# Loading the prompt as features by tokens, and dropping its transposes on TensorE

## The chip, the cores and the metric

The kernel runs on one core of a Trainium2 chip. The time is the device time of one execution in microseconds (us); for the kernel before the change it is the median of three runs, 3384.19 us (3377.82 to 3388.36). The engines are named as the profile names them: PE (TensorE; PEld is its weight load), DVE (VectorE), ACT (ScalarE), POOL (GpSimd) and SP (SyncE, which here only issues DMAs).

## The reference, cut to what matters

One inference step of a hybrid decoder layer. A prompt of 4096 tokens of 1024 features is normalised, multiplied by a weight of 1024 x 3072, and the twelve column blocks of the product feed four branches (a diagonal state-space model, a gated convolution, stick-breaking attention, attention to memory tokens). Beside it runs a decoding step of 8 x 4 tokens over a paged cache.

```
def rmsnorm(x, g):
    y = xf * lax.rsqrt(jnp.mean(xf * xf, axis=-1, keepdims=True) + EPS)
    return y * g
h = rmsnorm(x, lp["norm_g"]) @ lp["w_in"]
(a_u, a_g, b_b, b_c, b_x, b_g, c_q, c_k, c_v, c_g, m_q, m_g) = jnp.split(h, N_IN_BLOCKS, axis=-1)
```

The change concerns only how `rmsnorm(x, norm_g)` of the prompt comes to stand where the matrix product reads it.

## The kernel before, in words

The first stage projects the prompt. It goes through eight chunks of 512 tokens; within a chunk it goes through 24 units, one for each 128 of the 3072 output features. A unit (`part`, `proj`, L211 to L223) is 24 matmuls of 128 x 128 weights on 512 tokens: for each of eight 128-feature blocks `hi*hi` (L218), `hi*lo` (L219) and `lo*hi` (L220), since weights and input are each split in a rounded part and its remainder. The weights of unit i come by one DMA of 512 KB (`stg`, L204, two buffers), ACT copies the rounded part (`whl<-stg`, L42), and DVE subtracts it to make the remainder (`whl<-stg,whl`, L45, "the low part" below). The first L220 of a unit cannot start before that subtraction is done. The DMA for unit i+2 and the ACT copy for unit i+1 are issued in unit i.

The order on every engine is the order in which the program is written; nothing reorders it. `proj` calls `between` three times in a unit. `between` first runs what stands in the list `soon` (small pieces of work that were put off), then at most one of the low parts, then `slot`, which advances the decoding step and other background generators. So the projection's matmuls, the decoding step (`dz`, `dO`, `dwT`, cache loads `kt` from POOL's queue and `vt` from SP's queue) and the branches (`nat`, `pT`, `mo` and others) lie interleaved on all engines.

The input must stand with features on the 128 partitions, in a buffer `xh` (rounded part and remainder, 8 blocks, 512 tokens). Before the change the prompt is loaded as it lies, 128 tokens by 1024 features (`x_load`, L188, units 14 to 17 of the chunk before). `x_stats` (units 17 to 20) squares it on ACT in two halves that also give the sums, and scales it on DVE by the token's factor and the feature's weight (L179). `x_split` then transposes four 128 x 128 pieces on PE (L195) into a PSUM tile of the pool `tr` (two buffers, shared with `bc`, `yT`, `nat` and others), ACT copies the rounded part into `xh`, and DVE subtracts. There are eight such splits for a chunk, put between the matmuls of units 22 and 23 of the chunk before and units 0 and 1 of the chunk.

The second stage (from about 2000 us) is the attention over the prompt and the output projection; the change does not touch it.

Of the kernel before, what the change touches and what calls it, by code (L numbers as in the profile page):

```python
# [2 lines left out]

# [5 lines left out]
F32 = mybir.dt.float32  # L9
F32R = mybir.dt.float32r  # L10
I32 = mybir.dt.int32
AF = mybir.ActivationFunctionType
ALU = mybir.AluOpType
# [4 lines left out]
SEQ, DM, GW = 4096, 1024, 256  # L18
KT = DM // 128
CH = 512  # L20
NCH = SEQ // CH
EPS = 1e-6
A_U, A_G, B_B, B_C, B_X, B_G, C_Q, C_K, C_V, C_G, M_Q, M_G = range(12)

def dap(ap, off, dims):
    return bass.AP(tensor=ap.tensor, offset=ap.offset + off, ap=dims)
# [2 lines left out]
@with_exitstack  # L29
def hymba_kernel(ctx: ExitStack, tc: tile.TileContext, x_p, x_s, cache_k, cache_v, s_re, s_im, s_conv,  # L30
                 cmem_k, cmem_v, ptab, mem_p, norm_g, w_in, w_out, gng, lam_re, lam_im, b_re, b_im,
                 c_re, c_im, log_dt, ssm_d, w_glu, conv_w, sb_bias, w_mem, fin_g,
                 o_yp, o_ys, o_k, o_v, o_hre, o_him, o_conv, o_mk, o_mv, o_sk, o_sv,
                 o_shre, o_shim, o_sconv):
    nc = tc.nc
# [2 lines left out]
    mm, tr = nc.tensor.matmul, nc.tensor.transpose  # L38
    V, S, P, SP = nc.vector, nc.scalar, nc.gpsimd, nc.sync

    def act(out, in_, f=AF.Copy, **kw):
        return S.activation(out, in_, f, **kw)  # L42

    def tt(eng, out, a, b, op):
        return eng.tensor_tensor(out=out, in0=a, in1=b, op=op)  # L45

    cst = ctx.enter_context(tc.tile_pool(name="cst", bufs=1))
# [16 lines left out]
    ident = cst.tile([128, 128], F32, name="ident")  # L64
    jmat = cst.tile([128, 128], F32, name="jmat")
    ones32 = cst.tile([128, 32], F32, name="ones32")
    nhalf = cst.tile([128, 8], F32, name="nhalf")
    sel = cst.tile([128, 2], F32, name="sel")
    sgn = cst.tile([128, 1], F32, name="sgn")
    gnc = cst.tile([128, 8], F32, name="gnc")  # L70
    cwc = cst.tile([128, 2, 3], F32, name="cwc")
    b4 = cst.tile([128, 4], F32, name="b4")
    nb4 = cst.tile([128, 4], F32, name="nb4")
# [37 lines left out]
    sb = p1.enter_context(tc.tile_pool(name="sb1", bufs=1))  # L111
# [3 lines left out]
    def ev(dt=F32, name="ev"):  # L115
        return sb.tile([128, 512], dt, tag="ev", name=name, bufs=5)
# [7 lines left out]
    def trp(name="trp"):  # L124
        return ps.tile([128, 4, 128], F32, tag="tr", name=name, bufs=2)
# [45 lines left out]
    def x_stats(x, n=128, then=lambda f: f()):  # L171

        ss = sb.tile([128, 4], F32, tag="ss", name="ss", bufs=4)
        for k in range(2):
            act(ev()[0:n], x[0:n, k * 512:(k + 1) * 512], AF.Square, accum_out=ss[0:n, k:k + 1])
        tt(V, ss[0:n, 0:1], ss[0:n, 0:1], ss[0:n, 1:2], ALU.add)
        V.tensor_scalar(ss[0:n, 0:1], ss[0:n, 0:1], 1.0 / DM, EPS, op0=ALU.mult, op1=ALU.add)
        tt(P, ss[0:n, 2:3], ss[0:n, 0:1], nhalf[0:n, 0:1], ALU.pow)
        then(lambda: V.scalar_tensor_tensor(x[0:n], x[0:n], ss[0:n, 2:3], ngr[0:n], op0=ALU.mult, op1=ALU.mult))  # L179

    xq = {}

    def x_tile(name="xt", dt=F32):
        return sx.tile([128, DM], dt, tag="xt", name=name, bufs=4)

    def x_load(i):
        xq[i] = x_tile()
        SP.dma_start(xq[i], x_p[0, i * 128:(i + 1) * 128, :])  # L188

    def x_split(i, k4):  # L190
        xs = xq[i]
        t0 = i % 4 * 128
        t = trp("xT")
        for k in range(4):
            tr(t[:, k, :], xs[:, (k4 * 4 + k) * 128:(k4 * 4 + k + 1) * 128], ident)  # L195
        hi = xh[:, k4 * 4:k4 * 4 + 4, 0, t0:t0 + 128]
        act(hi, t)
        tt(V, xh[:, k4 * 4:k4 * 4 + 4, 1, t0:t0 + 128], t, hi.bitcast(F32), ALU.subtract)


    def w_load(col):

        stg = sb.tile([128, KT, 128], F32, tag="stg", name="stg", bufs=2)
        SP.dma_start(stg, w_in[col // 128])  # L204
        return stg
# [36 lines left out]
    def sample_turn(xt):  # L242
        t = trp("xT")
        for k in range(KT):
            tr(t[:, k // 4, k % 4 * 32:k % 4 * 32 + 32], xt[0:32, k * 128:(k + 1) * 128], ident[0:32, 0:32])
        V.tensor_copy(smpt[:, 0:256], t[:, 0:2, :].rearrange("p a b -> p (a b)"))
# [618 lines left out]
    def dec_index():  # L865
        SP.dma_start(ptr, ptab)
        rep = x_tile("rep", I32)
        SP.dma_start(rep, dap(ptab, 0, [[0, 128], [1, 1024]]))
        io = sb.tile([128, 1], I32, name="io")
        r3 = rep.rearrange("p (s k) -> p s k", s=8)  # L870
        for q in range(4):
            V.tensor_scalar(idxk[32 * q:32 * q + 32], r3[32 * q:32 * q + 32, :, 32 * q:32 * q + 32], 32, None,
                            op0=ALU.mult)
        P.iota(io, pattern=[[0, 1]], base=0, channel_multiplier=1)
        V.tensor_scalar(io, io, 31, None, op0=ALU.bitwise_and)
        tt(V, idxk.rearrange("p s g -> p (s g)"), idxk.rearrange("p s g -> p (s g)"),
           io.to_broadcast([128, 256]), ALU.add)
# [249 lines left out]
    xh = sb.tile([128, KT, 2, 512], F32R, name="xh")  # L1127
# [35 lines left out]
    def w_fetch(i):  # L1163
        if i < len(seq):
            _, blk, ft = seq[i]
            stgs[i] = w_load(blk * GW + ft * 128)

    def w_hi(i, eng=V):
        if i < len(seq):
            whls[i] = w_split(stgs[i], eng)  # L1170

    def w_sample(i):
        stg = stgs.pop(i)
        if seq[i][0] == 0:
            sample_proj(stg, *seq[i][1:])

    jobs, lows, soon = [], [], []

    def x_job():
        if jobs:  # L1180
            x_split(*jobs.pop(0))

    def catch_up():

# [83 lines left out]

    x_load(0)
    x_load(1)  # L1270
    SP.dma_start(ngr, dap(norm_g, 0, [[0, 128], [1, DM]]))
    w_fetch(0)
    x_load(2)
    w_fetch(1)
    xst = sample_load()
# [22 lines left out]
    def first():  # L1298
        yield from mset
        yield from setup  # L1300
# [5 lines left out]
    npc = len(order0)  # L1306
    i = 0
    while i < len(seq):
        c, k = divmod(i, npc)
        if k in (0, npc - 2):  # L1310

            for z in range(2):
                for j in range(2):
                    if z == j == 0:
                        if i:
                            w_sample(i)
                            w_fetch(i + 2)
                        w_hi(i + 1)
                    if i == z == 0 and j == 1:
                        sample_turn(xst)  # L1320
                        dec_index()
                        fast.append(first())
                        bg.extend(fast + [new_keys()])
                    if i == j == 0 and z:
                        w_sample(0)
                        w_fetch(2)
                    if z == j == 1:
                        w_sample(i + 1)
                        w_fetch(i + 3)
                        w_hi(i + 2)  # L1330
                    new = [4 * c + 2, 4 * c + 3] if (k, z, j) == (0, 0, 0) else \
                        [4 * c + 4, 4 * c + 5] if (k, z, j) == (npc - 2, 1, 0) and c + 1 < NCH else []
                    jobs.extend((t, k4) for t in new for k4 in range(2))
                    if j == 0 and i + z:
                        x_job()
                    part(i + j, z * 256, z * 256 + 256)
                    if j == 0:
                        x_job()
                    if z == 1:
                        post(i + j)  # L1340
                    slot()
            i += 2
        else:
            w_sample(i)
            w_fetch(i + 2)
            w_hi(i + 1)
            if 14 <= k < 18 and c + 1 < NCH:
                x_load(4 * c - 10 + k)
            if 17 <= k < 21 and c + 1 < NCH:
                x_stats(xq[4 * c - 13 + k], then=soon.append)  # L1350
            if c == NCH - 1 and k == 18:
                load_q(0, 0)
                load_keys(0, 0, 0, x_tile("k0", F32R).rearrange("p (l n) -> p l n", l=2))
            part(i, 0, 512)
            post(i)
            slot()
            i += 1
# [10 lines left out]
    sb = ctx.enter_context(tc.tile_pool(name="sb2", bufs=1, reuse_waits="tile"))  # L1368
# [505 lines left out]
    for i in range(nu + LAG + 1):  # L1874
        j = i - LAG
        z = None
        if i < nu:
# [7 lines left out]
            z = scores(*units[i])  # L1885
# [3 lines left out]
        if 0 <= j < nu:  # L1889
            ws, n = sa.pop(j)  # L1890
# [12 lines left out]
    while out_step(2.0) or bg:  # L1903
# [4 lines left out]
_INS = ['x_prompt', 'x_sample', 'cache_sb_k', 'cache_sb_v', 'state_ssm_re', 'state_ssm_im', 'state_conv',  # L1908
        'cache_mem_k', 'cache_mem_v', 'page_table', 'mem_prompt', 'norm_g', 'w_in', 'w_out', 'group_norm_g',
        'ssm_lambda_re', 'ssm_lambda_im', 'ssm_b_re', 'ssm_b_im', 'ssm_c_re', 'ssm_c_im', 'ssm_log_dt', 'ssm_d',  # L1910
        'ssm_w_glu', 'conv_w', 'sb_bias', 'w_mem_kv', 'final_norm_g']
_OUTS = [(1, 4096, 1024), (8, 4, 1024), (1, 1, 4096, 4, 64), (1, 1, 4096, 4, 64), (1, 1, 16, 64), (1, 1, 16, 64),
         (1, 1, 2, 256), (1, 1, 256, 4, 64), (1, 1, 256, 4, 64), (8, 1, 4, 4, 64), (8, 1, 4, 4, 64),
         (8, 1, 16, 64), (8, 1, 16, 64), (8, 1, 2, 256)]
# [2 lines left out]
def _lay(name, a):  # L1917

    if name in ('w_in', 'w_mem_kv'):
        return a.reshape(KT, 128, -1, 128).transpose(2, 1, 0, 3)  # L1920
    return a


# [19 lines left out]
```

## Time and profile before

| | |
|---|---|
| median of three runs | 3384.19 us |
| the profiled execution | 3391.03 us |
| its span on the core | 3389.3 us |
| mean granted clock of PE | 0.974 of full |
| PE busy | 3156.3 us, 93% of the span |
| DVE, ACT, POOL busy | 67%, 53%, 37% |
| mean DMA rate | 184 GB/s |

The profile is of one execution. Busy time of an engine is the union of its instructions. An idle stretch before an instruction is named by what ended it. Matmuls are pipelined: a matmul of 0.39 us is followed by the next after some 0.23 us, so what one costs is read from start to start. "Granted clock" is the share of TensorE's full clock in a stretch: 1.00 is the upper level of 2.4 GHz, 0.50 the lower of 1.2 GHz.

### The profile page before, as it was taken

To read this page: it belongs to the slowest core of one execution; us is meant where nothing else is said; L and a number is where in the kernel's file an instruction comes from. 1 tells how busy PE (TensorE), PEld (TensorE's weight loads), DVE (VectorE), ACT (ScalarE), POOL (GpSimd) and SP (SyncE) were. 2 spreads that over 40 slices of the span, in tenths; PEclk is the share of its full clock that TensorE was granted. 3 is DMA by queue.
4 is the path that set the end of the run, shared out by engine and by line. 5 is a ranking of instruction groups with operands and counts; after the bars stand their busy time and mean duration, and the time that the engine had idled before them with its cause. 6 is when DMAs were issued, how large, how long until landed. Compare 5 with 4: busy or idle time off the path is not lost. (4 is left out here: it accounts for less than half of the span.)

```text
span 3389.3 us, 65303 instructions
## 1 busy us (share of the span) xinstructions
PE 3156.3 (93%) x23383; PEld 2280.9 (67%) x23383; DVE 2278.2 (67%) x3628; ACT 1780.1 (53%) x3324; POOL 1252.3 (37%) x1721
## 2 busy tenths in 40 slices
PE   7888999999999999999999988999999888999998
PEld 6556767677767677676676666666666665666667
DVE  5885667666676675676756567777656777777773
ACT  3435444443544444444434456677656666667771
POOL 1466322122222122222223035555545555556550
PEclk8999999999999999999999979999989999999999
DMA  6667887888877878878888444333323223322213
GB/s 211 192 210 223 270 283 226 270 278 265 283 257 240 280 248 295 271 228 266 274 263 232 150 159 126 94 99 97 91 82 100 72 94 101 102 81 84 86 60 118
DMA packets 382179, 623.57 MB, mean 184 GB/s; under 512 B 54568, under 2 KB 245488, under 8 KB 381856
## 3 DMA queue, kind: packets, MB, share of 16 engines
q1 hardware_dynamic: 344912, 484.90, 45.3%
q0 software_dynamic: 36944, 134.50, 12.1%
q8 instruction: 186, 3.05, 0.4%
q14 instruction: 137, 1.12, 0.1%
HBM read 539.33 MB, written 79.95 MB: 183 GB/s over the span
## 5 line engine op out<-in xcount | busy, mean ns | idle before, releaser
L45 POOL TENSOR_TENSOR bt<-bt,T 128x512 f32<-128x512 f32 (+3 forms) x576 | 599.9, 1041 | 604.7 <-DVE T L1470 398.8
L218 PE MATMUL pj<-xh,whl 128*128 128x512 f32 (+1 forms) x1792 | 723.6, 404 | 0.0
L1470 DVE TENSOR_TENSOR_SCAN T<-om,cy,z 128x513 f32<-128x513 f32 x448 | 549.1, 1267 | 178.8 <-ACT bt L42 83.0
L220 PE MATMUL pj<-xh,whl 128*128 128x512 f32 (+1 forms) x1792 | 657.5, 367 | 9.5 <-DVE whl L45 9.5
L219 PE MATMUL pj<-xh,whl 128*128 128x512 f32 (+1 forms) x1792 | 656.5, 366 | 0.1
L888 POOL DMA_INDIRECT kt<-in_cache_sb_k_dram,idxk x256 | 298.0, 1164 | 900.3 <-DVE kT L1056 791.6
L218 PEld LDWEIGHTS pj<-xh,whl 128*128 128x128 f32 x1792 | 343.1, 191 | 120.2 <-issue 81.8
L42 ACT ACTIVATE wT<-wt 128x512 f32<-128x512 f32 (+3 forms) x360 | 193.0, 557 | 409.7 <-PE wt L1487 409.5
L220 PEld LDWEIGHTS pj<-xh,whl 128*128 128x128 f32 x1792 | 342.7, 191 | 70.3 <-DVE whl L45 12.4
L42 ACT ACTIVATE bt<-z,b 128x512 f32<-128x512 f32 (+3 forms) x576 | 383.6, 666 | 0.0
L42 ACT ACTIVATE om<-z,nb 128x512 f32<-128x512 f32 (+3 forms) x576 | 379.0, 658 | 6.9 <-DVE T L1470 4.1
L219 PEld LDWEIGHTS pj<-xh,whl 128*128 128x128 f32 x1792 | 344.5, 192 | 44.8 <-issue 8.6
L1449 PE MATMUL z<-kst,qst 64*128 64x512 f32 (+3 forms) x1704 | 302.1, 423 | 32.6 <-DVE T L1470 29.5
L1056 DVE STREAM_TRANSPOSE kT<-kt 128x1024 f32<-128x1024 f32 x256 | 315.2, 1233 | 16.3 <-DMA kt<-in_cache_sb_k_dram,idxk 14.3
L45 DVE TENSOR_TENSOR whl<-stg,whl 128x1024 fp32r<-128x1024 f32 x191 | 234.2, 1226 | 107.8 <-ACT whl L42 93.0
L1487 PE MATMUL wt<-ident,bt 128*128 128x128 f32 x2112 | 292.7, 280 | 3.3 <-DVE rr L1538 0.9
L1487 PEld LDWEIGHTS wt<-ident,bt 128*128 128x128 f32 x2112 | 242.5, 143 | 65.7 <-issue 40.8
L1503 PE MATMUL ya<-wT,vt 128*64 128x256 f32 (+1 forms) x2176 | 262.2, 382 | 0.3 <-DVE wT L1490 0.3
L1449 PEld LDWEIGHTS z<-kst,qst 64*128 64x128 f32 x1704 | 154.0, 190 | 140.4 <-issue 60.0
L42 ACT ACTIVATE whl<-stg 128x1024 fp32r<-128x1024 f32 x192 | 203.2, 1058 | 82.5 <-issue 35.5
L1560 PE MATMUL wo<-wo,mt 128*128 128x512 f32 x512 | 218.9, 427 | 2.2 <-ACT mt L42 2.2
L1562 PE MATMUL wo<-wo,mt 128*128 128x512 f32 x512 | 206.1, 402 | 0.7 <-DVE mt L45 0.7
(756 smaller groups left out, 4873.1 us busy)
## 6 DMA issues: line engine op xcount, KB each, us to landing
vt<-in_cache_sb_v_dram SPq DMA_DIRECT2D x1024, 128.0 KB
stg<-in_w_in_dram SPq DMA_DIRECT2D x192, 512.0 KB
kst<-kscr SPq DMA_DIRECT2D x71, 512.0 KB
xt<-in_x_prompt_dram SPq DMA_DIRECT2D x64, 512.0 KB
pkt<-pack_d SPq DMA_DIRECT2D x64, 449.0 KB
vt<-vscr SPq DMA_DIRECT2D x71, 256.0 KB
mr<-mscr SPq DMA_DIRECT2D x32, 512.0 KB
out_dram<-yb SPq DMA_DIRECT2D x32, 512.0 KB
```

Source lines behind the costliest of these rows:

```text
L42: return S.activation(out, in_, f, **kw)
L45: return eng.tensor_tensor(out=out, in0=a, in1=b, op=op)
L218: mm(o[:, t0:t1], hi[:, k, :], xh[:, k, 0, t0:t1], start=(k == 0), stop=False)
L219: mm(o[:, t0:t1], hi[:, k, :], xh[:, k, 1, t0:t1], start=False, stop=False)
L220: mm(o[:, t0:t1], lo[:, k, :], xh[:, k, 0, t0:t1], start=False, stop=(k == KT - 1))
L888: P.indirect_dma_start(out=kq[j], out_offset=None, in_=ck_rows, in_offset=bass.IndirectOffsetOnAxis(ap=idxk[:, u // NU, gg:gg + 1], axis=0))
L1056: V.transpose(kts[j], kq.pop(j))
L1449: mm(zs[h][:, 0:n], qs[r, lq_, qt * 128:(qt + 1) * 128], ks[r, lk, 0:n], start=(lq_ + lk == 0), stop=(lq_ == 1 and not diag))
L1470: V.tensor_tensor_scan(T[:, 0:n + 1][:, ::-1], om[:, 0:n + 1][:, ::-1], z[:, 0:1].to_broadcast([128, n + 1]), 1.0 if diag else c, op0=ALU. ...
L1487: tr(t[:, k, :], ws[h][:, k * 128:(k + 1) * 128], ident)
L1503: mm(ya[0][h * 64:h * 64 + 64, q0 * 128:(qt + 1) * 128], v[:, k, h * 64:h * 64 + 64], wTs[h][:, k, q0 - qt + 1:2, :].rearrange("p a b -> p ...
L1560: mm(o, mt[:, k, 0, :], wo[:, k, 0, cs], start=(k == 0), stop=False)
```

## The change

From the second chunk on, the prompt comes to the chip a second time, laid out on the host as (chunk, pair of feature blocks, 128 features, 2, 512 tokens), so that a plain load has features on the partitions (`xf_load`, four loads of 512 KB in units 14 to 17). The normalising factors still need sums over a token's features; so each group of 128 tokens is also loaded as it lies, in two halves of 256 KB (`xf_rms`, units 10 to 13), only to be squared on ACT. Four transposes of a broadcast column per chunk (`xf_bc`, unit 16) spread the 512 factors over all partitions, DVE scales the features (`xf_scale`, units 17 to 20), and `xf_split` makes the two parts of `xh` from SBUF with no work on PE. The first chunk is as before.

```diff
+    def xf_load(c, k2):
+        xf[c, k2] = x_tile("xf")
+        SP.dma_start(xf[c, k2], x_t[c, k2].rearrange("p k n -> p (k n)"))
+
+    def xf_rms(c, t):
+        if t == 0:
+            xr[c] = sb.tile([128, 4], F32, tag="xr", name="xr", bufs=1)
+        ss = sb.tile([128, 4], F32, tag="ss", name="ss", bufs=4)
+        i = 4 * c + t
+        for k in range(2):
+            xn = sb.tile([128, 512], F32, tag="xn", name="xn", bufs=3)
+            SP.dma_start(xn, x_p[0, i * 128:(i + 1) * 128, k * 512:(k + 1) * 512])
+            soon.append(functools.partial(act, xn, xn, AF.Square, accum_out=ss[:, k:k + 1]))
+
+        def rest():
+            tt(V, ss[:, 0:1], ss[:, 0:1], ss[:, 1:2], ALU.add)
+            V.tensor_scalar(ss[:, 0:1], ss[:, 0:1], 1.0 / DM, EPS, op0=ALU.mult, op1=ALU.add)
+            tt(P, xr[c][:, t:t + 1], ss[:, 0:1], nhalf[:, 0:1], ALU.pow)
+        soon.append(lambda: soon.append(rest))
+
+    def xf_bc(c):
+        t = trp("xbc")
+        for k in range(4):
+            tr(t[:, k, :], xr[c][:, k:k + 1].to_broadcast([128, 128]), ident)
+        xr[c] = sb.tile([128, 512], F32, tag="xbc", name="xbc", bufs=1)
+        act(xr[c], t.rearrange("p a b -> p (a b)"))
+
+    def xf_scale(c, k2):
+        for j in range(2):
+            x = xf[c, k2][:, j * 512:j * 512 + 512]
+            soon.append(functools.partial(V.scalar_tensor_tensor, x, x, ngc[:, 2 * k2 + j:2 * k2 + j + 1], xr[c],
+                                          op0=ALU.mult, op1=ALU.mult))
+
+    def xf_split(c, k2, h):
+        x = xf[c, k2].rearrange("p (k n) -> p k n", k=2)[:, :, h * 256:h * 256 + 256]
+        hi = xh[:, 2 * k2:2 * k2 + 2, 0, h * 256:h * 256 + 256]
+        act(hi, x)
+        tt(V, xh[:, 2 * k2:2 * k2 + 2, 1, h * 256:h * 256 + 256], x, hi.bitcast(F32), ALU.subtract)
...
+    SP.dma_start(ngc, dap(norm_g, 0, [[1, 128], [128, 8]]))
     w_fetch(0)
...
-            if 14 <= k < 18 and c + 1 < NCH:
-                x_load(4 * c - 10 + k)
-            if 17 <= k < 21 and c + 1 < NCH:
-                x_stats(xq[4 * c - 13 + k], then=soon.append)
+            if c + 1 < NCH:
+                if 10 <= k < 14:
+                    xf_rms(c + 1, k - 10)
+                if 14 <= k < 18:
+                    xf_load(c + 1, k - 14)
+                if k == 16:
+                    xf_bc(c + 1)
+                if 17 <= k < 21:
+                    xf_scale(c + 1, k - 17)
...
+    if name == 'x_features':
+        return a.reshape(NCH, CH, KT // 2, 2, 128).transpose(0, 2, 4, 3, 1)
```

On ACT, in units 11 and 12 of the third chunk, this stood before (`whl<-stg` is the copy of the next unit's weights; `dwT`, `om` and `dbt` belong to the decoding step, `ev<-pj` takes a finished unit out of PSUM):

```order
L42 ACTIVATE whl<-stg 128x1024
L42 ACTIVATE dwT<-dz 128x128
L42 ACTIVATE om_127<-dz,bdc 128x2x4x32
L42 ACTIVATE dbt<-dz,bdc 128x2x4x32
L42 ACTIVATE ev<-pj 128x512
L42 ACTIVATE ev<-pT 128x512
L42 ACTIVATE whl<-stg 128x1024
```

And this stands there now:

```order
L43 ACTIVATE whl<-stg 128x1024
L43 ACTIVATE xn,ss<-xn 128x512 x2
L43 ACTIVATE dwT<-dz 128x128
L43 ACTIVATE om_128<-dz,bdc 128x2x4x32
L43 ACTIVATE dbt<-dz,bdc 128x2x4x32
L43 ACTIVATE ev<-pj 128x512
L43 ACTIVATE ev<-pT 128x512
L43 ACTIVATE whl<-stg 128x1024
L43 ACTIVATE xn,ss<-xn 128x512 x2
```

The two squares of a freshly loaded `xn` stand right behind the weight copy of the unit that issues their loads; before, no instruction there read the prompt.

On DVE, in units 11 and 12 of the same chunk, this stood before (`whl<-stg,whl` is the low part; `ev<-nat` a transposed piece on its way to DRAM; `kT` a piece of the decoding step's keys):

```order
L45 TENSOR_TENSOR dw<-dbt,dT 128x256
L45 TENSOR_TENSOR whl<-stg,whl 128x1024
L332 COPY ev<-nat 128x512
L1056 STREAM_TRANSPOSE kT<-kt 128x1024
L45 TENSOR_TENSOR whl<-stg,whl 128x1024
```

And this stands there now:

```order
L46 TENSOR_TENSOR dw<-dbt,dT 128x256
L46 TENSOR_TENSOR ss<-ss 128x1
L211 TENSOR_SCALAR ss<-ss 128x1
L46 TENSOR_TENSOR whl<-stg,whl 128x1024
L376 COPY ev<-nat 128x512
L1100 STREAM_TRANSPOSE kT<-kt 128x1024
L46 TENSOR_TENSOR ss<-ss 128x1
L211 TENSOR_SCALAR ss<-ss 128x1
L46 TENSOR_TENSOR whl<-stg,whl 128x1024
```

The two small operations on the sums, which read what the squares wrote, have moved from units 17 to 20 to units 10 to 13, and stand in front of each unit's low part.

## Rows read from the trace of the kernel before

**Rows 1.** The page's first line.

```profile
span 3389.3 us, 65303 instructions
```

**Rows 2.** Windows, the first stage past its start: busy time by engine, granted clock, DMA.

```profile
core 0: us, PE busy (x) PEld busy (x) DVE busy (x) ACT busy (x) POOL busy (x), PEclk, DMA share, GB/s
...
600.00:1800.00 1200.00, 1166.59 (x9636) 862.70 (x9635) 794.66 (x1328) 536.38 (x1019) 282.40 (x343) 0.99 0.82 266
```

**Rows 3.** Timeline of PE, two splits at a chunk's start: start, duration, instruction, [idle before].

```profile
786.41 0.66 PE L195 MATMUL xT<-ident,xt 128*128 128x128 f32 x4
786.82 0.37 PE L218 MATMUL pj<-xh,whl 128*128 128x256 f32 x1
...
801.74 0.66 PE L195 MATMUL xT<-ident,xt 128*128 128x128 f32 x4
804.16 0.62 PE L307 MATMUL bc<-ident,rr 128*128 128x128 f32 x4 [1.76 <-DVE xh L45]
```

**Rows 4.** Waits of PE from 560 to 1985 us: total, times, longest.

```profile
PE bc L307 <- DVE xh L45: 6.5, 3, 2.6
...
PE yT L682 <- DVE xh L45: 2.4, 4, 1.0
```

**Rows 5.** The tile `xT`: duration in ns min/median/max, first and last start.

```profile
L195 PE MATMUL xT<-ident,xt x256: 270/273/476, 9.5 to 1733.4; 128*128 128x128 f32 x128
```

**Rows 6.** The tile `xt`: the squares and the scaling.

```profile
L42 ACT ACTIVATE ev<-xt x66: 612/618/660, 4.3 to 1688.4; 128x512 f32<-128x512 f32 x64, 32x512 f32<-32x512 f32 x2
...
L179 DVE SCALAR_TENSOR_TENSOR xt<-xt,ss,ngr x33: 1273/1284/1646, 8.1 to 1690.9; 128x1024 f32<-128x1024 f32 x32, 32x1024 f32<-32x1024 f32 x1
```

**Rows 7.** Timelines of SP and ACT at the kernel's start.

```profile
0.82 0.87 SPq L188 DMA_DIRECT2D xt<-in_x_prompt_dram  x2
...
4.29 0.63 ACT L42 ACTIVATE ev<-xt 128x512 f32<-128x512 f32 x1 [2.20 <-DMA xt<-in_x_prompt_dram]
```

**Rows 8.** Timeline of SP, third chunk, units 11 to 13.

```profile
685.63 0.82 SPq L204 DMA_DIRECT2D stg<-in_w_in_dram  x1
...
688.72 6.62 SPq L903 DMA_DIRECT2D vt<-in_cache_sb_v_dram  x8
695.44 1.49 SPq L204 DMA_DIRECT2D stg<-in_w_in_dram  x1
...
703.99 0.40 SPq L204 DMA_DIRECT2D stg<-in_w_in_dram  x1
```

**Rows 9.** Timeline of DVE there, and its busy time up to 702.83.

```profile
685.15 1.22 DVE L45 TENSOR_TENSOR whl<-stg,whl 128x1024 fp32r<-128x1024 f32 x1
687.06 0.69 DVE L332 COPY ev<-nat 128x512 f32<-128x512 f32 x1 [0.69 <-PE nat L330]
...
693.44 1.22 DVE L45 TENSOR_TENSOR whl<-stg,whl 128x1024 fp32r<-128x1024 f32 x1 [4.53 <-ACT whl L42]
...
694.66:702.83 8.17, 4.86 (x10) 1.00 0.63 194
```

**Rows 10.** Timeline of PE there: the first L220 of units 12, 13 and 14.

```profile
692.26 0.40 PE L220 MATMUL pj<-xh,whl 128*128 128x512 f32 x1
...
702.40 0.40 PE L220 MATMUL pj<-xh,whl 128*128 128x512 f32 x1
...
711.12 0.39 PE L220 MATMUL pj<-xh,whl 128*128 128x512 f32 x1
```

**Rows 11.** SP and PE, fourth chunk: two weight loads, the L220 of units 12, 13.

```profile
904.83 0.46 SPq L204 DMA_DIRECT2D stg<-in_w_in_dram  x1
913.71 0.39 PE L220 MATMUL pj<-xh,whl 128*128 128x512 f32 x1
...
920.19 0.38 SPq L204 DMA_DIRECT2D stg<-in_w_in_dram  x1
925.66 0.40 PE L220 MATMUL pj<-xh,whl 128*128 128x512 f32 x1
```

**Rows 12.** Windows around an idle stretch of PE in the fourth chunk.

```profile
926.00:932.00 6.00, 3.98 (x36) 2.89 (x34) 2.63 (x4) 5.97 (x14) 0.94 (x1) 1.00 0.98 341
932.00:939.00 7.00, 6.19 (x42) 3.74 (x43) 2.90 (x4) 1.24 (x3) 1.11 (x1) 0.51 0.55 152
```

More of the change, by code (lines that the diff above doesn't have):

```diff
@@ L1 @@
+import functools
 import math
@@ L31, in hymba_kernel @@
                  cmem_k, cmem_v, ptab, mem_p, norm_g, w_in, w_out, gng, lam_re, lam_im, b_re, b_im,
-                 c_re, c_im, log_dt, ssm_d, w_glu, conv_w, sb_bias, w_mem, fin_g,
+                 c_re, c_im, log_dt, ssm_d, w_glu, conv_w, sb_bias, w_mem, fin_g, x_t,
                  o_yp, o_ys, o_k, o_v, o_hre, o_him, o_conv, o_mk, o_mv, o_sk, o_sv,
@@ L70, in hymba_kernel @@
     gnc = cst.tile([128, 8], F32, name="gnc")
+    ngc = cst.tile([128, 8], F32, name="ngc")
     cwc = cst.tile([128, 2, 3], F32, name="cwc")
@@ L188, in x_load @@
         SP.dma_start(xq[i], x_p[0, i * 128:(i + 1) * 128, :])
+    xf, xr = {}, {}
+    def xf_load(c, k2):
[31 more added lines that the diff above has]
+        tt(V, xh[:, 2 * k2:2 * k2 + 2, 1, h * 256:h * 256 + 256], x, hi.bitcast(F32), ALU.subtract)
     def x_split(i, k4):
@@ L1180, in x_job @@
         if jobs:
-            x_split(*jobs.pop(0))
+            jobs.pop(0)()
     def catch_up():
@@ L1330, in hymba_kernel @@
                         w_hi(i + 2)
-                    new = [4 * c + 2, 4 * c + 3] if (k, z, j) == (0, 0, 0) else \
-                        [4 * c + 4, 4 * c + 5] if (k, z, j) == (npc - 2, 1, 0) and c + 1 < NCH else []
-                    jobs.extend((t, k4) for t in new for k4 in range(2))
+                    if (i, z, j) == (0, 0, 0):
+                        jobs.extend(functools.partial(x_split, t, k4) for t in (2, 3) for k4 in range(2))
+                    elif (k, z, j) == (0, 0, 0):
+                        jobs.extend(functools.partial(xf_split, c, k2, 1) for k2 in range(4))
+                    elif (k, z, j) == (npc - 2, 1, 0) and c + 1 < NCH:
+                        jobs.extend(functools.partial(xf_split, c + 1, k2, 0) for k2 in range(4))
                     if j == 0 and i + z:
@@ L1910 @@
         'ssm_lambda_re', 'ssm_lambda_im', 'ssm_b_re', 'ssm_b_im', 'ssm_c_re', 'ssm_c_im', 'ssm_log_dt', 'ssm_d',
-        'ssm_w_glu', 'conv_w', 'sb_bias', 'w_mem_kv', 'final_norm_g']
+        'ssm_w_glu', 'conv_w', 'sb_bias', 'w_mem_kv', 'final_norm_g',
+        'x_features']
 _OUTS = [(1, 4096, 1024), (8, 4, 1024), (1, 1, 4096, 4, 64), (1, 1, 4096, 4, 64), (1, 1, 16, 64), (1, 1, 16, 64),
@@ L1932 @@
     arrays, args = {}, []
+    inputs = dict(inputs, x_features=inputs['x_prompt'])
     for name in _INS:
```

## Prediction

> **What bounds the kernel now.** I read the windows first. From 600 to 1800 us, five of the seven chunks that the change touches, PE is busy 1166.6 of 1200 us, while DVE is at 66%, ACT at 45% and the DMA engines at 0.82 [rows 2]. So this stage ends when PE's in-order stream ends. Work taken off PE there shortens the kernel by its start-to-start cost, and whatever makes PE wait there lengthens it one for one. The other engines have spare time, but each also works its own queue in order, so what counts is when PE's inputs are ready, above all the low part of the next unit's weights. Next I read the timelines around a chunk's start, where the splits are, and around units 10 to 14, where the new loads will stand.
>
> **What goes from PE.** The four transposes of a split have a median duration of 273 ns each [rows 5], but they overlap: the next matmul starts 0.41 us after the first of them [rows 3], so a split costs PE 0.41 us. Per chunk eight go and one like them comes (`xbc`), in seven chunks: 7 x 7 x 0.41 = 20 us off.
>
> With the transposes goes their use of the two PSUM buffers. PE waited for DVE's split to release one of them: `bc` 6.5 us and `yT` 2.4 us [rows 4], an example being the 1.76 us ahead of `bc` [rows 3]. The splits now read SBUF, so these go: 9 us off. What is late next there is the split itself, ACT copy and DVE subtraction, whose number and size stay; I take them as equal from SBUF. The gain is 29 us (bounds: 20 if other waits take their place, 29 plus little else, since PE has only 33 us idle in the 1200).
>
> The Trainium skill ("TensorE: Matmul & The Clock Gate", Part 4: PE-mode transpose) puts a transpose at about 275 ns in a kernel's context. The durations agree, the spacing does not. By the rule 7 x 28 transposes x 0.275 would be 54 us rather than 20.
>
> **What is hidden.** DVE scales 8 halves per chunk instead of 4 tiles of 1.28 us [rows 6]: between nothing and 1 us per chunk more, on an engine at 66%. One ACT copy per chunk for `xbc` is one square's size, 0.62 us [rows 6], at 45%. SP issues 8 more loads per chunk at 0.43 us, since two took 0.87 [rows 7]; in front of the first weights there is one more, 0.4 us. The second copy of x is 2.1 MB per chunk: at 266 GB/s with a share of 0.82 [rows 2] the engines can do 324, so it takes 6.5 us of a chunk's 240 (five of them in these 1200 us) and lifts the share to about 0.85. I count nothing; were DMA the bound it would be 7 x 6.5 = 45 us.
>
> **What is added to PE's path: a loop over four queues.** In units 10 to 13 SP issues the weights for unit i+2, then both halves of 128 tokens. ACT's squares of them stand behind the weight copy of the same unit, and DVE's two small sums stand before the low part of unit i+1. So that low part now waits for a DMA issued in its own unit, and behind it waits the `nat` copy, for which SP waits before it issues eight cache loads and the next weights. Before, the loads were three units ahead of their squares.
>
> How long is this? At the kernel's start a load of 512 KB issued at 0.82 let ACT go at 4.29 [rows 7], so 3.5 us with nothing else in flight. The two halves follow 512 KB of weights: 0.52 MB at 324 GB/s is 1.6 us more, so 5.1, and I take 5.2 us from the weights' issue to the landing. Bounds: 3.5 if all overlaps; 8.4 if 1 MB of cache loads is ahead too (1.05 MB at 324, 3.2 us). Then one square 0.6 [rows 6], 0.5 that I allow for the sum's read-out and the small operations, and 1.22 for the low part [rows 9]: it is done 7.5 us after the weights' issue (5.8 to 10.7).
>
> Third chunk, unit 11: weights issued at 685.63 [rows 8], low part done at 693.1. PE wants it at 692.26 [rows 10]: PE waits 0.9 us. Before, it was done at 686.4 [rows 9].
> Unit 12: the `nat` copy ended at 687.75 [rows 9] and now at 693.8, 6.1 us later. The eight cache loads occupy SP from 688.72 to 695.34 without a pause and the next weights go right behind [rows 8], so these slip by 6.1, to 701.5. Low part done at 709.0; PE wants it at 702.40 + 0.9: PE waits 5.7.
> Unit 13: DVE has 4.9 us of work between the low part and the end of the next `nat` copy [rows 9], which ends at 713.9 rather than 702.83, 11.1 later, and the weights of 703.99 [rows 8] slip to 715.1. Low part at 722.6, PE wants it at 711.12 + 6.6: PE waits 4.9.
> That is 11.5 us in this chunk.
>
> The fourth chunk has longer units. Unit 11: 904.83 + 7.5 = 912.3 against 913.71, no wait; unit 12: 920.19 + 7.5 = 927.7 against 925.66, 2 us [rows 11]. I take 3, since SP slips a little there as well. The source tells chunks with an even number from the odd ones (the state-space work), so I count three chunks like the third and three like the fourth, and nothing for the first, whose units last longer: 3 x 11.5 + 3 x 3 = 43.5 us.
>
> Each long wait also costs clock. PE was busy 4.0 of 6 us in one stretch, and in the next 7 us the granted clock was 0.51, nearly all at the lower level [rows 12]: 3.5 us of full-speed work lost. I take 2 us for each of the six waits of about 5 us: 12 (0 to 21).
>
> **The sum.** -20 - 9 + 43.5 + 12 = +26.5 us on the profiled execution's 3391.0 (a span of 3389.3 [rows 1] and 1.7 around it): 3417.5. That execution lies 6.8 above the median of 3384.2, so I forecast 3411.
>
> The Trainium skill ("DMA: Bandwidth & Descriptors", Rules for kernel authors) advises to issue a DMA early and wait on it late; this change does it the other way for the squares. Its fit for one DMA (Anatomy of one DMA) of 2.0 us plus bytes/436e3 would land the 1.05 MB after 4.4 us, an estimate, rather than 5.2: then about 9 us in each of three chunks, and 3400 in all. The row at the start, 3.5 us for 0.52 MB, is 0.3 above the fit.
>
> **Rivals.**
> *The loads land in time.* SP may run further ahead of PE than in the two chunks that I followed; the squares then cost ACT nothing and the low parts stay early (5.9 us early in unit 11 before) [rows 9, 10]. It speaks for this that PE's time is the bound, and a slower PE gives SP time; against it, that SP issued the weights only 6.6 us ahead of PE's need. It decides where landing plus 2.3 us is under that distance in all units. -29 on 3384: 3355. This is the faster side. With the skill's 275 ns it would be 3322.
> *The loop damps.* With 3.5 us to the landing, the same chain gives 0, 3.2 and 3.2 us in the third chunk and about 0.3 in the fourth: 20 us, clock 4, gain 29: 3379, no change that can be told.
> *The loop winds up.* With 8.4 us it gives 4.1, 8.9 and 8.1 us, and 5 in the fourth: 79, clock 21, gain 29: 3455. DVE's held queue also keeps back `kT`, and POOL's factor stands before its key gathers, which speaks for this; against it, that DMA has 0.18 free.
>
> **How the numbers follow.** Forecast case 0.42, in time 0.18, damped 0.20, winding up 0.20. Less than 0.3% (10 us) cannot be told from no change. Faster: the first rival and a third of the damped, 0.24. Same: half of the damped and the forecast's lower edge, 0.13. Slower: 0.63. The forecast's own range is 3392 to 3435; for 8 in 10 I go to 3353 and 3460, which leaves out the far ends of the outer two.
>
> **What would show it.** No `xT` transposes after the first chunk and one group of `xbc` per chunk; from start to start, a chunk's first units shorter by some 4 us. Against that, ACT's `xn` idle on the DMA of `xn`, 1 to 5 us each, DVE's `ss` on ACT, and PE's L220 (its new line) on DVE `whl` or `ss`, some 44 us where it was small; SP's weight loads in units 12 and 13 later in their unit than before; granted clock below 0.99 in these units. I am wrong if ACT's wait for `xn` is short, or long while PE does not wait; or if PE waits at another place, such as `dz` for `kT`.

## The result, and the profile after

The change made the kernel slower, and by far more than forecast.

| | before | after |
|---|---|---|
| median, four runs each | 3382.38 us (3377.82 to 3388.36) | 3533.16 us (3532.04 to 3535.99) |
| ratio to before, 95% interval | | 1.0449 (1.0431 to 1.0468) |
| the profiled execution | 3391.03 us | 3535.99 us |
| mean granted clock of PE | 0.974 | 0.955 |
| last matmul of the projections ends at | 1972.7 us | 2117.5 us |

The last row places the loss: the first stage ends 144.8 us later and the spans differ by 145.0, so the second stage took the same time. First the page's first line and the window that answers to [rows 1, 2] (PE, PEld, DVE, ACT and POOL busy, granted clock, DMA share, GB/s):

```profile
span 3534.3 us, 65024 instructions
...
600.00:1800.00 1200.00, 1079.74 (x8612) 789.09 (x8611) 719.78 (x1215) 497.43 (x948) 265.17 (x300) 0.95 0.77 249
```

Every engine is less busy than before and the DMA engines too: nobody works more, everybody waits. The waits from 300 to 1900 us, one group per engine (waiting instruction, releaser: total us, times, longest):

```profile
ACT xn L43 <- DMA xn<-in_x_prompt_dram: 169.2, 24, 15.2
...
DVE ss L46 <- ACT xn L43: 183.7, 24, 12.8
...
POOL xr L46 <- DVE ss L211: 179.8, 21, 12.1
...
SPq L380 <- DVE ev L376: 172.6, 18, 14.4
```

These are the four links of the predicted loop, and they stand in units 10 to 13 of each chunk but the last: 24 waits of ACT in the six chunks that lie in the window. SP's wait is for the `nat` copy; in the same window before it was:

```profile
SPq L336 <- DVE ev L332: 53.5, 14, 7.4
```

PE's waits, 560 to 1985 us, answering to [rows 4]:

```profile
PE nat L374 <- ACT p L43: 24.1, 3, 9.2
PE dz L1128 <- ACT dbt L43: 23.4, 5, 7.4
PE nat L374 <- ACT Ya L43: 21.9, 2, 13.4
PE pj L264 <- DVE whl L46: 15.8, 9, 3.8
PE pj L262 <- DVE ev L46: 13.5, 5, 3.5
```

The waits of `bc` and `yT` for the split are gone, as predicted. The low part (L264) is a place of waiting, as predicted, but only the fourth: PE's longest waits are at `nat` and `dz`, for ACT's `p`, `Ya` and `dbt`. `Ya` and `dbt` stand in ACT's queue behind a square which waits for its load. `p` is held through DVE: it needs DVE's `mx` (L835, L836), which stands behind the waiting sum and the low part. Here are DVE's sum and, after `mx`, ACT's first instruction for `p`, a table load, in the third chunk:

```profile
746.88 0.16 DVE L46 TENSOR_TENSOR ss<-ss 128x1 f32<-128x1 f32 x1 [12.42 <-ACT xn L43]
...
749.26 1.28 ACT L43 ACT_TABLE_LOAD   x1 [1.93 <-DVE mx L836]
```

The fourth chunk, where I had counted 3 us, shows the loop best. SP, ACT, DVE and PE in units 11 and 12, answering to [rows 11]:

```profile
965.97 0.46 SPq L248 DMA_DIRECT2D stg<-in_w_in_dram  x1
966.48 1.57 SPq L206 DMA_DIRECT2D xn<-in_x_prompt_dram  x2
982.49 0.39 SPq L380 DMA_DIRECT2D out_dram<-ev  x1
983.45 6.84 SPq L947 DMA_DIRECT2D vt<-in_cache_sb_v_dram  x8
990.39 0.38 SPq L248 DMA_DIRECT2D stg<-in_w_in_dram  x1
```

```profile
975.72 0.63 ACT L43 ACTIVATE xn<-xn 128x512 f32<-128x512 f32 x1 [10.34 <-DMA xn<-in_x_prompt_dram]
...
995.05 0.63 ACT L43 ACTIVATE xn<-xn 128x512 f32<-128x512 f32 x1 [10.80 <-DMA xn<-in_x_prompt_dram]
...
996.29 2.02 ACT L43 ACTIVATE Ya<-yT 128x512 f32<-128x512 f32 x2
```

```profile
977.11 0.16 DVE L46 TENSOR_TENSOR ss<-ss 128x1 f32<-128x1 f32 x1 [9.83 <-ACT xn L43]
...
977.38 1.22 DVE L46 TENSOR_TENSOR whl<-stg,whl 128x1024 fp32r<-128x1024 f32 x1
...
981.78 0.68 DVE L376 COPY ev<-nat 128x512 f32<-128x512 f32 x1
```

```profile
978.65 0.80 PE L264 MATMUL pj<-xh,whl 128*128 128x512 f32 x1 [3.48 <-DVE whl L46]
997.42 1.12 PE L374 MATMUL nat<-ident,ev 128*128 128x128 f32 x4 [13.41 <-ACT Ya L43]
```

Follow it from queue to queue. The load issued at 966.48 lets ACT go at 975.72, 9.2 us later. DVE's sum waits for that, then the low part (done at 978.6, PE waits 3.48), then the `nat` copy, done at 982.46. SP had waited for that copy since 968.05; it stores, issues eight cache loads and comes to the next weights at 990.39, 24.4 us after the last ones (15.4 before [rows 11]). Directly behind stands the next `xn`, whose square ACT has been waiting for since 984. The `Ya` copies are queued behind the square, and PE stands still for 13.41 us. Windows over this chunk's unit 12 (columns as above):

```profile
984.00:1011.00 27.00, 13.59 (x95) 9.03 (x95) 7.51 (x13) 8.48 (x19) 4.51 (x4) 0.75 0.68 218
```

PE is busy half the time, and the clock granted is 0.75.

### The profile page after: what moved, and what is told of

Its sections match the earlier page's. It is cut to its first block, busy times and chain, and to the rows that moved or that the text cites. A ratio compares the mean times of both kernels' runs of the same rounds, so it can differ in the third digit from the quotient of the medians.

```text
span 3534.3 us, 65024 instructions
## 1 busy us (share of the span) xinstructions
PE 3177.4 (90%) x23187; PEld 2284.6 (65%) x23187; DVE 2285.3 (65%) x3656; ACT 1782.9 (50%) x3331; POOL 1270.9 (36%) x1721
## 5 line engine op out<-in xcount | busy, mean ns | idle before, releaser
L262 PE MATMUL pj<-xh,whl 128*128 128x512 f32 (+1 forms) x1792 | 733.7, 409 | 13.5 <-DVE ev L46 13.5
L264 PE MATMUL pj<-xh,whl 128*128 128x512 f32 (+1 forms) x1792 | 669.9, 374 | 27.3 <-DVE whl L46 27.3
L263 PE MATMUL pj<-xh,whl 128*128 128x512 f32 (+1 forms) x1792 | 666.4, 372 | 1.5 <-DVE xh L46 1.4
L262 PEld LDWEIGHTS pj<-xh,whl 128*128 128x128 f32 x1792 | 352.4, 197 | 139.8 <-issue 87.8
L264 PEld LDWEIGHTS pj<-xh,whl 128*128 128x128 f32 x1792 | 351.0, 196 | 90.7 <-DVE whl L46 31.9
L263 PEld LDWEIGHTS pj<-xh,whl 128*128 128x128 f32 x1792 | 353.2, 197 | 47.3 <-issue 7.9
```

The costliest lines, as they stand in the source:

```text
L262: mm(o[:, t0:t1], hi[:, k, :], xh[:, k, 0, t0:t1], start=(k == 0), stop=False)
L263: mm(o[:, t0:t1], hi[:, k, :], xh[:, k, 1, t0:t1], start=False, stop=False)
L264: mm(o[:, t0:t1], lo[:, k, :], xh[:, k, 0, t0:t1], start=False, stop=(k == KT - 1))
```

## The experiments

Each ratio is to runs of the kernel before on the same chip, with its 95% interval. Theory 1: waiting for a load issued in the same unit is the whole loss. Its rivals: the extra traffic, the new work, the buffers.

**1. Without the loads.** The squares read a resident tile:

```diff
-            xn = sb.tile([128, 512], F32, tag="xn", name="xn", bufs=3)
-            SP.dma_start(xn, x_p[0, i * 128:(i + 1) * 128, k * 512:(k + 1) * 512])
-            soon.append(functools.partial(act, xn, xn, AF.Square, accum_out=ss[:, k:k + 1]))
+            soon.append(functools.partial(act, ev(), ngr[:, k * 512:(k + 1) * 512], AF.Square,
+                                          accum_out=ss[:, k:k + 1]))
```

> The changed kernel without the loads of `xn`: the squares read a resident tile (`ngr`) instead, so the row factors are not those of x. All else of the change stays (loads by features, scaling, splits from SBUF, `xbc`). Theory 1, the added time is the wait for data loaded in the same unit: all of it goes and the gain of 29 us is left, 3345 to 3365 us, with no unit 10 to 13 longer than before. Rival 2, reading x from SBUF, the extra work on DVE and POOL, or PE's wait for `xbc` cost the time: 3480 to 3535.

Measured: 3381.56 us, 0.9982 (0.9965 to 0.9999). The loss is gone, so rival 2 falls. But only some 6 us are left of the expected gain of 29, and the time lies above theory 1's range; experiments 8 to 13 look for the rest.

**2. With the loads, nobody waiting.** Only the last line of the edit above; the loads stay.

> The changed kernel with all 56 loads of `xn` issued where they are, but the squares read a resident tile, so nobody waits for these loads (the row factors are not those of x). Theory 1, the wait costs the time: 3350 to 3370 us, within 10 us of the run without these loads. Rival 3, the bytes (14.7 MB more) or the 56 further issues on SP cost it: 3450 to 3530; were DMA the bound and only bytes counted, 45 us more than without the loads.

Measured: 3378.39 us, 0.9973 (0.9958 to 0.9987). Level with experiment 1, though above the stated range like it. Rival 3 falls: 56 more issues and 14.7 MB cost nothing that can be told. The DMA share of 600 to 1800 us is 0.85, what the prediction had worked out.

**3 and 4. ACT alone waits; DVE alone waits.** First, the sums two units later:

```diff
+    rests = []
...
-        soon.append(lambda: soon.append(rest))
+        rests.append(rest)
...
+                if 12 <= k < 16:
+                    soon.append(rests.pop(0))
```

> The changed kernel with DVE's small sums and POOL's factor put off by two units; loads and ACT's squares stay where they are. So ACT still waits for the fresh load, DVE and POOL no longer do. Theory 1a, the loop goes over DVE (low part and `nat` copy late, SP late): it is cut, 3360 to 3420 us. Theory 1b, ACT's held queue alone does it (PE waits at `nat` and `dz` for ACT's copies, and these make DVE and SP late): 3480 to 3535.

Then the resident squares of experiment 1 with a DVE operation that reads the fresh load (`x2` holds its two halves):

```diff
         def rest():
+            tt(V, ss[:, 2:3], x2[0][:, 0:1], x2[1][:, 0:1], ALU.add)
             tt(V, ss[:, 0:1], ss[:, 0:1], ss[:, 1:2], ALU.add)
```

> The changed kernel with the squares reading a resident tile (the row factors are not those of x) and DVE, at the place of its small sums, reading one column of each half of the fresh `xn`. So DVE waits for the fresh load and ACT does not. Theory 1a, the loop over DVE and SP is what costs: 3470 to 3535 us. Theory 1b, ACT's hold costs: 3355 to 3420.

Measured: 3485.69 us, 1.0292 (1.0258 to 1.0325), and 3493.87 us, 1.0314 (1.0288 to 1.0340). Neither of 1a and 1b holds alone. Either wait closes a loop, and costs over 100 us more than experiment 2; both together cost 161 (1.0449 less 0.9973, of 3382), not the sum. PE's main waits up to 2120 us say how they differ. With ACT waiting:

```profile
PE nat L376 <- ACT Ya L43: 33.5, 3, 12.9
PE dz L1130 <- ACT dbt L43: 29.5, 10, 8.0
```

With DVE waiting:

```profile
PE pj L268 <- DVE whl L46: 26.6, 16, 6.0
PE nat L378 <- ACT p L43: 22.5, 3, 8.0
```

At `nat` PE waits 4.8 us for `p` in the first run and 22.5 in the second, since `p` needs DVE's `mx`. The prediction had followed the second loop only, and of it only the low part; the first, through ACT's queue to PE's `nat` and `dz`, is as dear.

**5 to 7. The same loads, 0, 1 and 3 units earlier**, into the four large buffers, which lie idle in these units (shown for one unit; `xn_load` holds the two loads, the squares stay in 10 to 13):

```diff
+                if 9 <= k < 13:
+                    xn_load(c + 1, k - 9)
                 if 10 <= k < 14:
                     xf_rms(c + 1, k - 10)
```

> The changed kernel with the same loads of `xn` in the same units 10 to 13, but into the four large buffers that lie idle there (one of 128 x 1024 per unit) rather than three small ones that take turns. Output is the reference's. Theory 1 (the wait is for the load's own time, buffers have no part): 3520 to 3540 us. Rival 4 (SP waits until a square has given back one of the three small buffers): 3380 to 3480.

> As the run with the large buffers, and the loads of `xn` one unit earlier (9 to 12); the squares stay in units 10 to 13. Theory 1: the landing, 4 to 10 us after the issue, fits mostly into one unit of 8 to 14 us, so most of the 152 us above the run without these loads goes: 3385 to 3430 us. If the place of the loads in SP's queue is what costs: 3480 to 3530.

> As the run with the large buffers, and the loads of `xn` three units earlier (7 to 10), as far ahead of the squares as the loads of x were before the change. Output is the reference's. Theory 1: no wait is left, 3375 to 3390 us, level with the run without these loads (3381.6). Rival: the loads collide with other transfers where they stand now, or a buffer in the first chunk is not free: 3390 to 3440.

Measured: 3532.20 us, 1.0424 (1.0388 to 1.0460); 3375.32 us, 0.9963 (0.9947 to 0.9980); 3383.33 us, 0.9999 (0.9979 to 1.0018). The buffers have no part. One unit earlier takes the whole loss away, more than the 3385 to 3430 that I expected: no wait of ACT for `xn` is left. So the time from issue to landing is not dear in itself; it is dear where what waits for the load stands in front of the work that lets SP issue the next ones. Three units are no better than one.

The Trainium skill ("DMA: Bandwidth & Descriptors", Rules for kernel authors) says to issue a DMA early and wait for it late, so that its fixed cost overlaps. The trace agrees, with a larger price than a fixed cost: 157 us between 3532.2 and 3375.3 for one unit.

**8. The worth of the transposes alone.** In the kernel before, the splits read x as it lies in SBUF, so the transposes are left out and the projections get x in the wrong layout:

```diff
-        t = trp("xT")
-        for k in range(4):
-            tr(t[:, k, :], xs[:, (k4 * 4 + k) * 128:(k4 * 4 + k + 1) * 128], ident)
+        t = xs[:, k4 * 512:k4 * 512 + 512].rearrange("p (a b) -> p a b", a=4)
```

> The kernel before with nothing changed but that the splits read x as it lies in SBUF, without its transposes on TensorE (so the projections get x in the wrong layout). It measures by itself what the transposes' going is worth. The prediction's step (0.41 us for each of 64 groups, and the 9 us of waits for PSUM buffers): 26 + 9, so some 3350 us. Rival, as the run without the loads of `xn` lets expect: PE arrives earlier at the chunk's first units and waits there for the weights and the splits instead, 3370 to 3382.

Measured: 3378.34 us, 0.9971 (0.9958 to 0.9985), 10 us instead of 35. Windows from 0 to the end of the last projection, first the kernel before, then this one:

```profile
0.00:1972.70 1972.70, 1863.84 (x15152) 1380.31 (x15152) 1296.20 (x2338) 865.74 (x1647) 539.56 (x650) 0.98 0.77 247
```

```profile
0.00:1962.00 1962.00, 1838.49 (x14897) 1355.38 (x14897) 1299.82 (x2338) 862.71 (x1646) 542.24 (x650) 0.98 0.78 248
```

PE's busy time falls by 25.3 us, for 64 groups 0.40 us each: the prediction's 0.41 holds. But PE idles 123.5 instead of 108.9 us, 14.6 more. The Trainium skill ("TensorE: Matmul & The Clock Gate", Part 4: PE-mode transpose) has about 275 ns for one in one kernel's context, so 1.1 us for a group of four one behind the other, by an estimate from it. The duration agrees, a median of 273 ns [rows 5], but the four overlap: in this stream the measurement decides, 0.40 for a group.

Where PE idles shows at the fourth chunk's start, here on SP, ACT, DVE and PE in turn:

```profile
782.81 0.97 SPq L309 DMA_DIRECT2D mscr<-Yb  x2
785.18 6.25 SPq L901 DMA_DIRECT2D vt<-in_cache_sb_v_dram  x8
791.54 0.38 SPq L202 DMA_DIRECT2D stg<-in_w_in_dram  x1
```

```profile
796.86 1.06 ACT L42 ACTIVATE whl<-stg 128x1024 fp32r<-128x1024 f32 x1 [2.60 <-DMA stg<-in_w_in_dram]
797.82 1.65 ACT L42 ACTIVATE xh<-xt 128x512 fp32r<-128x512 f32 x3
```

```profile
798.47 0.69 DVE L45 TENSOR_TENSOR xh<-xt,xh 128x512 fp32r<-128x512 f32 x1 [3.88 <-ACT xh L42]
799.08 0.68 DVE L45 TENSOR_TENSOR ev<-pj,ev 128x512 f32<-128x512 f32 x1
```

```profile
799.91 0.55 PE L216 MATMUL pj<-xh,whl 128*128 128x256 f32 x1 [3.07 <-DVE ev L45]
```

The weights are issued behind a store of `Yb` and eight cache loads; ACT's copy waits for them, the splits wait behind the copy, the gate's product `ev` behind a split, and PE for the PSUM buffer that `ev` reads. Before, PE was still at the transposes here, and the same copy waited less:

```profile
799.41 1.06 ACT L42 ACTIVATE whl<-stg 128x1024 fp32r<-128x1024 f32 x1 [0.67 <-DMA stg<-in_w_in_dram]
```

The transposes had lain in this gap.

**9 and 11. A third buffer for the weights**, on the kernel of experiment 6 and on the kernel before (`bufs=2` to `bufs=3` for `stg`):

> The kernel with `xn` one unit early (3375.3 us), and a third buffer for the weights as they land, in the room that the small `xn` buffers gave back. If the weights' late landing at the chunk's first units is what eats the gain of the transposes (ACT's weight copy waits for its load there, the splits stand behind it) and SP was held by the two buffers: 3345 to 3365. If SP comes late for another reason, its own queue's waits: 3368 to 3380.

> The kernel before with a third buffer for the weights: the control for the run that has both. 3378 to 3390 if the buffers held nothing up while the transposes were there; 3350 to 3370 if they did anyway.

Measured: 3374.83 us, 0.9960 (0.9948 to 0.9972), and 3389.01 us, 1.0000 (0.9988 to 1.0012). A third buffer alone gains nothing in either kernel, so two buffers were not what held the weights.

**10. The `xbc` transposes in the middle of unit 16**, on the kernel of experiment 6 (`soon.append(functools.partial(xf_bc, c + 1))`):

> The kernel with `xn` one unit early, and the four transposes of the row factors (`xbc`) put into the middle of unit 16 instead of its start, where PE waited 7.6 us in all for ACT to give back the PSUM buffer. 3366 to 3374 if that wait goes, 3373 to 3378 if it only moves.

Measured: 3374.65 us, 0.9961 (0.9947 to 0.9975), level with experiment 6: nothing that can be told.

**12 and 13. The weights issued ahead of the store and the cache loads**, with the third buffer, in the pairs of units around a chunk's start; on the kernel of experiment 6, and on the kernel before:

```diff
                             w_fetch(i + 2)
+                            w_fetch(i + 3)
                         w_hi(i + 1)
...
-                        w_fetch(i + 3)
+                        if i == 0:
+                            w_fetch(i + 3)
                         w_hi(i + 2)
```

> The kernel with `xn` one unit early and three weight buffers (3374.8 us), and in each pair of units around a chunk's start the second weight load is issued together with the first, half a pair sooner, so ahead of the `Yb` store and the eight cache loads that stood before it in SP's queue. If the late weights at a chunk's start are what eats the transposes' gain: ACT's waits for weights, 28 us in 560 to 1985, go to under 8, PE's wait for DVE's `ev` (13 us) goes, and the time is 3350 to 3366. If another chain of nearly the same length (the splits, the merge) is behind it: 3368 to 3378.

> The kernel before with the same two edits of the weight loads (third buffer, second load of a pair issued with the first): the control. If the transposes filled time that PE would wait for the weights anyway, the kernel before gains little by it: 3378 to 3390. If PE was held there with the transposes too: 3360 to 3376.

Measured: 3354.26 us, 0.9907 (0.9885 to 0.9929), and 3379.40 us, 0.9981 (0.9966 to 0.9996). Between the two, the whole change is now worth 25 us by the medians (some 9 either way, an estimate from the two intervals), and 15.9 us by the end of the last projection in the two profiled executions (1943.5 and 1959.4 us). The kernel of experiment 12 is 0.9% faster than the kernel before. SP in experiment 12, the weights of two units ahead of the store and the cache loads at the fourth chunk's start:

```profile
765.45 0.84 SPq L254 DMA_DIRECT2D stg<-in_w_in_dram  x2
772.51 0.97 SPq L361 DMA_DIRECT2D mscr<-Yb  x2
774.91 7.09 SPq L953 DMA_DIRECT2D vt<-in_cache_sb_v_dram  x8
```

ACT's wait for weights and PE's for `ev`, 560 to 1985 us, in experiment 9 and then in 12:

```profile
ACT whl L43 <- DMA stg<-in_w_in_dram: 28.1, 15, 5.2
...
PE pj L268 <- DVE ev L46: 13.1, 5, 3.9
```

```profile
ACT whl L43 <- DMA stg<-in_w_in_dram: 10.2, 7, 4.0
...
PE pj L268 <- DVE ev L46: 0.5, 2, 0.3
```

PE's wait went as expected; ACT's fell to 10.2, not under 8. Whether the order would do it without the third buffer is not shown.

## Why the prediction was wrong

The direction was right, and so was the loop over four queues, but a second one runs beside it, and the loop, its clock cost and the gain all had the wrong size. For the sums, windows from 0 to the end of the last projection: the changed kernel, experiment 1, experiment 12.

```profile
0.00:2117.50 2117.50, 1885.63 (x14956) 1384.86 (x14956) 1302.92 (x2366) 866.98 (x1653) 556.88 (x650) 0.95 0.74 237
```

```profile
0.00:1961.10 1961.10, 1844.47 (x14956) 1365.25 (x14956) 1303.19 (x2366) 867.49 (x1654) 551.45 (x650) 0.98 0.78 248
```

```profile
0.00:1943.50 1943.50, 1843.48 (x14956) 1362.83 (x14956) 1301.80 (x2366) 866.77 (x1654) 553.37 (x650) 0.98 0.80 258
```

**The loop: +43.5 predicted, 115 measured.** The changed kernel idles PE for 231.9 us and experiment 1 for 116.6. Three steps of that term failed.

- *The landing.* I took 7.5 us from the weights' issue to the end of the low part. In the trace the median of the 28 units is 9.8 us (7.4 to 14.0). The upper bound of 10.7 was the better end for the middle. In the 24 units in which ACT stood waiting, the square starts a median 6.4 us after the weights' issue (4.4 to 9.8), where I had 5.2; from there to the end of the low part it is 2.9, where I had 2.3 with one square: the sum needs both. The 3.5 us at the kernel's start was also misread: six more loads were issued while that one was under way, so it was not one "with nothing else in flight". The fit of the Trainium skill ("DMA: Bandwidth & Descriptors", Anatomy of one DMA) that the prediction set beside this is given there for DMAs that GpSimd issues, and SP issues these; its 4.4 us were further off than my 5.2.
- *Only the low part held PE.* I followed DVE's queue as far as the low part and counted nothing for ACT's copies behind a waiting square, nor for `p`, which needs `mx` from behind DVE's sum. Experiment 3, where DVE does not wait, still loses 105 us against experiment 1 (1.0292 less 0.9982, of 3382). "Dz for `kT`" was named as a place that would prove me wrong; it was `dz` for `dbt`, and `nat` for `p` and `Ya`.
- *The fourth chunk stands for three with 3 us each, the first for nothing.* From the start of one chunk to the next, the changed kernel takes longer than experiment 1 by 16.7 us in the first; 28.1, 19.9 and 17.6 in the second, fourth and sixth; 24.7, 23.7 and 26.6 in the third, fifth and seventh. "SP slips a little there as well" was the wrong sentence: a slip of SP delays the next `xn`, and so itself. My slack was read from a schedule that the loop does not keep.

The rival that winds up, 3455 us, had nearly the right landing, but the other two errors as well: only the low part, and 5 us in a fourth chunk.

**The clock: +12 predicted, 41 measured.** The same 14956 matmuls keep PE busy 1885.6 us against 1844.5. The term was sized as 2 us for each of six waits; PE has 28 idle stretches of over 3 us in the changed kernel and 10 in experiment 1. The measured ratio of clock cost to idle time is 0.36; the prediction's was 0.28.

**The gain: -29 predicted, -6 to -13 delivered** (experiments 1, 6 and 8). The step "work taken off PE there shortens the kernel by its start-to-start cost" failed. The sizes were right: PE busy falls by 19.4 us in experiment 1 (20 predicted). But idle time rose by 7.8 instead of falling by 9, since at a chunk's start the weights set the pace, by SP's queue. I had read PE's 33 us of idle time in 1200 as proof that PE was the bound everywhere [rows 2]; a stretch where PE is busy with the transposes can still be one in which it has nothing more urgent to do.

From start to start the two places of the splits come apart. Units 22 and 23 of the eight chunks together take 153.5 us before and 131.2 in experiment 1; units 0 and 1 take 164.3 before and 181.3. So the gain came in full at a chunk's end, and the sign that I had named, a chunk's first units shorter by some 4 us, failed: together they became 17 us longer. Windows over units 0 and 1 of the third chunk, before, in experiment 1 and in experiment 12:

```profile
579.49:599.14 19.65, 19.65 (x177) 16.63 (x176) 11.44 (x16) 7.25 (x12) 2.81 (x3) 1.00 0.75 247
```

```profile
564.35:590.42 26.07, 21.22 (x164) 17.32 (x164) 13.77 (x21) 7.16 (x12) 4.25 (x4) 0.87 0.77 236
```

```profile
567.34:587.00 19.66, 18.94 (x165) 15.52 (x165) 13.67 (x21) 7.04 (x12) 4.62 (x4) 1.00 0.92 295
```

In experiment 12 these first units take 155.0 us in all, and against before the stage is 29.2 us shorter, 20.4 of it busy and 8.8 idle time. That this is the predicted 29 is in part luck. The edit of the weight loads helps the kernel before as well: against experiment 13 the stage is 15.9 us shorter, 13.9 busy and 2.0 idle. And two things that I had not counted are in it. `xbc` was priced at 0.41 us; in experiment 1 PE also waits 2.5 us for ACT's `p` ahead of it in the second, fourth and sixth chunk. And in unit 19 of the first chunk, which takes 16.3 us before and 14.7 in experiments 8 and 13, the change takes waits away that had nothing to do with the transposes, and leaves 9.5 in experiment 1. DVE's scaling of x had waited there for POOL's factor, and PE for `kT` behind it; DVE and PE, before:

```profile
286.99 1.28 DVE L179 SCALAR_TENSOR_TENSOR xt<-xt,ss,ngr 128x1024 f32<-128x1024 f32 x1 [1.97 <-POOL ss L45]
...
289.58 0.63 PE L1084 MATMUL dz<-kT,qbd 128*16 128x128 f32 x16 [2.82 <-DVE kT L1056]
```

**What held.** The waits of `bc` and `yT` went; the extra bytes and issues cost nothing (experiment 2); DVE's and ACT's added work, the wait ahead of `xbc` apart, cost nothing that can be told (experiment 1); the second stage did not move. "The loads land in time" would have needed one more unit of lead (experiment 6).

Left open: why three units of lead are some 8 us slower than one. Unit 8 of the third, fifth and seventh chunk is 3.0, 1.9 and 1.3 us longer there, and PE waits 2.6, 1.6 and 2.0 us in it for an `ev` from ACT, but no run tells the cause apart.

## What to carry to other kernels

A wait added to an in-order queue costs what stands behind it on that engine and, if one of those things lets the issuing queue go on, it feeds itself: look for a ring of queues before adding up single waits, and follow it through every engine that waits, not only the first. Here one unit of lead broke the ring. And before counting work off the busiest engine as gain, ask at that place which queue brings its next input; busy time there may only be filling a gap, which can then be closed from the other side.

## What the runs showed of the hardware that was not expected

Where ACT stood waiting, the load of 256 KB behind a load of weights let its square go 4.0 to 9.2 us after its issue, at a mean DMA share of 0.77, where the kernel's start had shown 3.5 for 512 KB with six loads behind it [rows 7]. And a part of the loss that no wait shows is TensorE's clock: 41 of the 156 us by which the stage is longer than in experiment 1, with 0.75 granted over 27 us in which PE was busy half the time.
